# A hybrid encoder layer on one core: the next input's loads move to GpSimd, and two groups of the first pass go last, by seven products

## The chip, the cores and the metric

The kernel runs on one core of a Trainium2 chip. The metric is the device time in microseconds (us) of one execution; of several runs the median is given. TensorE (PE) multiplies matrices, with a queue of weight loads beside it (PEld); VectorE (DVE), ScalarE (ACT) and GpSimd (POOL) do elementwise work; SyncE (SP) issues most transfers (DMAs); GpSimd and ScalarE issue some. Every engine works through its own list of instructions in order, and waits for others by semaphores. An instruction that waits holds up all that stands behind it on its engine.

## The reference

One encoder layer over 2048 tokens of width 1024:

```python
y = rmsnorm(h, norm_mix_g) @ w_in                      # q, k, v (512 each) and two halves of 512 for the convolution
att = dilated_sliding_attention(q, k, v)               # 8 heads, 3 patterns (window, dilation): (128,1) (512,4) (2048,16)
conv = conformer_conv(a, g, conv_w, ...)               # gated, 31 taps along the tokens, layernorm, silu
h = h + concatenate([att, conv]) @ w_out
h = h + softmax(xq xk^T / 16) xv @ w_xo                # cross-attention to 256 memory tokens, 4 heads
u = rmsnorm(h, norm_mlp_g) @ w_up                      # 1024 -> 4096
h = h + square(relu(u)) @ w_down                       # 4096 -> 1024
out = rmsnorm(h, norm_final_g)
```

All is in float32. The kernel keeps each operand as two fp16 parts, a high and a low one, and makes a product of three matmuls (`mm3`: high·high, high·low, low·high; lines 374 to 376). In the profile a name that ends in h or l is such a part.

## The kernel before

**Stages.** First the memory tokens are projected and x is normalised and transposed (to about 130 us), then come the linear layers for q, k, v and the convolution's input, and the first attention (to about 670 us). Then the 2048 tokens go in four passes of 512 (`post(p)`), each with the same stages: the mixed input times `w_out` (matmuls called `o`), the scores of cross-attention (`xs`), its output (`x`), the MLP, and the final norm. TensorE's products in these stages are `x[features] x tokens`: a weight tile of 128×128 is loaded, and 512 or 256 tokens stream through it.

**The MLP.** The 4096 hidden columns are eight groups of 512. Two groups are made (`up`), then multiplied by `w_down` (`dn`), four times in a pass. `orders[p]` says in which order the groups come. A group is made in one of two ways. A *whole* group takes four weight tiles of 1024×128 (`ws_u`), 96 matmuls of 512 columns on a plain input `y` (in pass 0), or 192 of 256 columns on an input in block columns (the whole groups of pass 1). The other way, `quad`, treats weights and input as 2×2 blocks and takes seven products in place of eight (Strassen's scheme): weights that were combined in advance lie in DRAM as `ust[fg][0..6]` and come as tiles `ws_t`, and the input comes in block columns B11, B12, B2, T1, T32, T4, of 256 tokens each, that hold blocks and sums of blocks. Seven products are 168 matmuls of 256 columns. `columns` makes those tiles and `put_columns` fills them, on VectorE and ScalarE, while the stage `x` runs.

**Weights.** In pass 0 a weight comes from DRAM in float32 (`raw_u`, `raw_d`), is split in two parts by ScalarE (L361) and VectorE (L362) into one of four buffers, and for later passes some are saved to DRAM (`wst`). In later passes they are loaded from `wst` or `ust` into one of seven buffers (`wtile`). The combined weights are made by `prep`, a generator with 24 steps in pass 0: it loads two tiles `pw`, forms sums on VectorE, splits them on ScalarE (L1548) and VectorE (L1551), and stores the parts (`give`, `step`). In pass 0 it prepares groups 0 and 1, whose stores SyncE issues; in passes 1 and 2 the other six, with GpSimd's issues. The first group by seven products before this change is in pass 1.

**Side work.** While TensorE does pass p, the attention (`att`) and the convolution (`conv`) of the tokens of pass p+1 are woven in: `weave` takes one step of the main generator and then, for each side, as many steps as its rate says. Their results are stored to DRAM (`cath`, `catl`, from tiles `cacc`, `cth`, `lhl`), and `load_pair` loads them back as the input of the next pass, 16 loads of 128 KB for each pass; a load waits for its store to land. They are issued by SyncE (a load reads cath<-cath in the profile, a store cath<-cacc).

**The early linear layers.** `lead` starts the first two of the units (`glu`: a scale for the weights, a load, a split) while the memory's last products still run, and `pipeline` goes on with the rest, with some steps ahead of each unit's products. `done` says how many steps the first two have had.

The order of the instructions on each engine is set when the program is built: a scheduler simulates a timeline and places each instruction, so a change at one place can move rows at another. The lines that the change touches are those of `pipeline`, `lead`, `att`, `load_pair`, `columns`, `quad`, and the loops of `post`.

Of the kernel before, what the change touches and what calls it, by code (L numbers as in the profile page):

```python
# [34 lines left out]
KC = D // P  # L35
# [13 lines left out]
def hybrid_layer(ctx, tc, A, out):  # L49
    nc = tc.nc  # L50
    ACT, DVE, POOL, PE = nc.scalar, nc.vector, nc.gpsimd, nc.tensor
# [5 lines left out]
    def dma(o, i, q=None):  # L57
        return (q or nc.sync).dma_start(o, i)
# [634 lines left out]
            if k < KC - 1:  # L693
                yield

    def pipeline(*units, done=0):

        def go(i, n=1):
            for _ in range(n if i < len(units) else 0):
                next(units[i])  # L700

        for i, n in enumerate((4, 3, 1)):
            go(i, n - done if i < 2 else n)
        for i, u in enumerate(units):
# [265 lines left out]
    with ExitStack() as st:  # L970
        sp = pool("stage", stack=st)
        setup0()
        mg = memory(sp)
        next(mg)
        next(mg)
        setup()
        xp = xprep(sp, (0, 1))
        alln = tuple(range(NG))
        early01 = (0, 1)
        weave(islice(mg, 12), (xp, 0.34))  # L980
        weave(islice(mg, 23), (xp, 0.65))
        units = [u for c in range(3) for u in glu(c, early01)]
        units += [lin_qk(isq, c) for c in range(4) for isq in (False, True)]

        def lead():

            next(units[0])
            next(units[1])
            for u in units[:2]:
                next(u)  # L990
                next(u)
                yield

        weave(mg, (xp, 0.65), (lead(), 0.5))
        drain(xp)
        banks["mm"] = (0, 1, 2, 5, 6)
        steps = pipeline(*units, *glu(3, early01), lin_v(0, alln), lin_v(1, early01), done=3)
        qkl = qk_load()
        next(steps)
        later = xprep(sp, (2, 3))  # L1000
        weave(islice(steps, 9), (later, 2.2), (qkl, 1.2))
        drain(later, qkl)
# [146 lines left out]
    cats = {}  # L1149
# [74 lines left out]
    def att_units(p, far, then):  # L1224
# [78 lines left out]

        load_v(0, (2, 1, 0) if far else (0, 1))
        nxt = None if far else load_keys(0, p)
        if p == 1:
            yield None
        for pr in range(H // 2):
            o0 = aq.tile([P, 4, 2, ROW], F32, tag="o0", name=f"o0_{p}{pr}", bufs=2)
# [110 lines left out]
    with ExitStack() as st:  # L1420
# [5 lines left out]
        rest = pinned(pipeline(*frest[:2], lin_v(1, (2, 3), True, True), *frest[2:], ahead(0), ahead(1), done=2), "pe")  # L1426
        for _ in range(38):
            next(rest)

# [72 lines left out]
    def load_pair(p, half, j):  # L1502
        for q, src in (("h", cath), ("l", catl)):
            for e in range(2):
                k = 4 * (1 - half) + 2 * j + e
                dma(cats[p][q, k], src[k][:, 512 * p:512 * (p + 1)])

    def resid_linear(load, rhs, korder, resid, hs, ssum, scale, gains, y, name, steps=False, wide=False, put=None):

# [89 lines left out]

    ready = set()  # L1600
    preps = {0: (0, 1), 1: (3, 5, 6, 7), 2: (4, 2)}
    orders = {0: range(8), 1: (0, 1, 2, 4, 3, 5, 6, 7), 2: (0, 1, 3, 5, 6, 7, 4, 2)}
    whole = {0: tuple(range(8)), 1: (2, 4), 2: ()}
    prepping = {}

    def columns(p):

        names = {"B11": 0, "T1": 1, "T4": 2}
        if p == 1:
            names["B12"] = 7  # L1610
        one = {(n, q): yp.tile([P, 4, 256], F16, tag=f"y{q}{i}", name=f"{n}{q}{p}") for n, i in names.items() for q in "hl"}
        two_ = {(n, q): [yp.tile([P, 2, 2, 256], F16, tag=f"y{q}{i + x}", name=f"{n}{q}{p}{x}") for x in range(2)]
# [46 lines left out]
    def quad(p, fg, src, sink, rsb):  # L1659

        def tile(i):
            t = wtile(f"t{p}{fg}{i}", 7, (P, 8, P))
            dma(flat(t), ust[fg][i])
            return t
# [50 lines left out]
    def post(p):  # L1715
# [72 lines left out]
                yield  # L1788
        banks["S"] = (3, 4)

        src = put = None
        if p:
            one, two_, src = columns(p)
            put = put_columns(one, two_, hs)
            y = None
        else:
            y = ytiles("m")
        ssum = ssum_tile(f"x{p}")
        xl = resid_linear(lambda m: wpost(bscr[m], f"b{p}{m}", S_B), pr_, list(range(KC)), lambda m: hs[m], hs, ssum, K_B,
                          gxm[:, 8:16], y, f"x{p}_", True, put=put)  # L1800
        for _ in range(3):
            next(xl)
            if late:
# [38 lines left out]
        for g in range(FG // 2):  # L1842
# [3 lines left out]
            for i, fg in enumerate(fgs):  # L1846
# [5 lines left out]
                ks = (0, 1, 2, 3, 4, 5, 6, 7)  # L1852
                if fg not in whole[p]:
                    while fg not in ready:
                        next(prepping[p])
                    yield from main_quad or quad(p, fg, src, into(ht), rsb)
                    ks = (0, 1, 2, 3, 6, 7, 4, 5)
                    continue
                for c in range(4):
                    wh, wl = wpost(wcols(w_up, fg * 512 + c * P), f"u{p}{fg}_{c}", S_UP, (P, 8, P),  # L1860
                                   4 * fg + c if fg in whole[1] else None, p)
                    pt = ps("mm", "up")
                    for z in range(2 if src else 0):
                        for k in range(KC):
                            n = f"B{1 + k // 4}{1 + z}"
                            mm3(halved(pt)[:, z], wh[:, k, :], wl[:, k, :], src[n]("h", k % 4), src[n]("l", k % 4),
                                k == 0, k == KC - 1)
                    for k in range(0 if src else KC):
                        mm3(pt, wh[:, k, :], wl[:, k, :], y["h", k], y["l", k], k == 0, k == KC - 1)

                    def finish(pt, j):

# [228 lines left out]
    for p in range(NG):  # L2101
# [8 lines left out]
        if p + 1 < NG:  # L2110
# [67 lines left out]
```

## Time and profile before

| | |
|---|---|
| median of 3 runs | 2642.85 us (2641.27 to 2646.11) |
| the profiled execution's own time | 2648.63 us |
| its span | 2646.4 us |
| TensorE busy | 2588.9 us, 98% |
| VectorE, ScalarE, GpSimd busy | 1946.5, 1241.8, 279.9 us |
| mean granted clock of TensorE | 0.993 |
| pass 0: `o` from 668, `x` from 771, first `up` from 821, `dn` from 868, 961, 1058, 1151 | us from the span's start |
| pass 1: `x` from 1338, first `up` from 1382, last `dn` from 1659 | us |

The profile is one execution. "Idle before" is time in which an engine stood still ahead of an instruction, with the work that released it. Matmuls overlap, so a matmul of 512 columns is recorded as 0.38 us long, while the next one starts 0.22 us after it.

### The profile page before, as it was taken

The numbers are of one execution on the slowest core, as the hardware profiler recorded it, in microseconds if no ns is written. First come the engines' busy times: TensorE is split into PE (matmuls) and PEld (weight loads), VectorE is DVE, ScalarE is ACT, GpSimd is POOL, SyncE is SP. The second block draws the span as 40 slices with busy tenths as digits, with TensorE's granted clock in tenths as the row PEclk, the third lists the DMA queues.
The fourth block names the chain that finished last, engine by engine and source line by source line (L and its number), as shares of the span: only waits on it lengthen the run. The fifth ranks groups of instructions, "written<-read, shape, count | busy, mean of one in ns | idle before, by whom it ended". The sixth has DMA issues, their size and how long they took to land. (4 is left out here: it accounts for less than half of the span.)

```text
span 2646.4 us, 45524 instructions
## 1 busy us (share of the span) xinstructions
PE 2588.9 (98%) x17710; PEld 1650.2 (62%) x17710; DVE 1946.5 (74%) x3775; ACT 1241.8 (47%) x2194; POOL 279.9 (11%) x369
## 2 busy tenths in 40 slices
PE   7999999999999999999999999999999999999998
PEld 7844448767555545545576677455776664468876
DVE  5896656567767999775799996467899556675566
ACT  5747545476555344554553344256443234452323
POOL 1134101132100010100011111000110000000000
PEclk9999999999999999999999999999999999999999
DMA  8987968666634757885367678454686465345442
GB/s 264 297 271 218 289 227 260 193 183 180 177 102 133 212 171 221 237 271 172 112 212 218 194 237 253 143 163 131 215 263 192 141 207 167 97 135 168 159 137 80
DMA packets 406361, 509.51 MB, mean 193 GB/s; under 512 B 81181, under 2 KB 301265, under 8 KB 405376
## 3 DMA queue, kind: packets, MB, share of 16 engines
q1 hardware_dynamic: 387728, 452.64, 56.4%
q0 software_dynamic: 13232, 44.94, 5.3%
q10 hardware_dynamic: 5184, 9.01, 0.9%
q8 instruction: 139, 2.28, 0.4%
q14 instruction: 78, 0.64, 0.1%
HBM read 390.75 MB, written 115.75 MB: 191 GB/s over the span
## 5 line engine op out<-in xcount | busy, mean ns | idle before, releaser
L391 DVE SCALAR_TENSOR_TENSOR cacc<-cu,cw,cacc 128x512 f32<-128x512 f32 x480 | 364.2, 764 | 5.4
L374 PE MATMUL dn<-hhh,ws_d 128*128 128x512 f16 x768 | 289.0, 381 | 8.7 <-DMA ws_d<-wst 5.6
L375 PE MATMUL dn<-hhl,ws_d 128*128 128x512 f16 x768 | 291.6, 381 | 0.6 <-DVE hhl L1655 0.6
L376 PE MATMUL dn<-hhh,ws_d 128*128 128x512 f16 x768 | 291.3, 381 | 0.0
L1039 DVE CUSTOM_DVE_ANT_0 sm<-s,mask,qks 128x256 f32<-128x256 f32 (+1 forms) x384 | 150.8, 433 | 35.4 <-PE s L1080 31.1
L1040 ACT ACTIVATE sm<-sm,o 128x256 f32<-128x256 f32 (+1 forms) x288 | 119.4, 455 | 112.1 <-DVE o L1039 111.7
L1050 DVE TENSOR_TENSOR pl<-pt,ph 128x512 f16<-128x512 f32 x160 | 109.5, 684 | 45.8 <-ACT ph L1049 45.4
L1049 ACT CAST ph<-pt 128x512 f16<-128x512 f32 x160 | 91.7, 573 | 101.1 <-PE pt L1046 101.0
L1903 DVE SCALAR_TENSOR_TENSOR h<-dn,bd,h 128x512 f32<-128x512 f32 x96 | 71.4, 745 | 83.5 <-PE dn L376 83.0
L375 PEld LDWEIGHTS <-ws_t 128*128 128x128 f16 x1232 | 120.7, 98 | 18.6 <-issue 3.0
L376 PEld LDWEIGHTS <-ws_d 128*128 128x128 f16 x768 | 75.3, 98 | 90.6 <-issue 2.5
L374 PEld LDWEIGHTS <-ws_t 128*128 128x128 f16 x1232 | 120.9, 98 | 17.3 <-DMA ws_t<-ust 0.6
L376 PEld LDWEIGHTS <-ws_t 128*128 128x128 f16 x1232 | 120.8, 98 | 17.1 <-issue 1.1
L374 PEld LDWEIGHTS <-ws_d 128*128 128x128 f16 x768 | 75.3, 98 | 88.4 <-DMA ws_d<-wst 5.8
L375 PEld LDWEIGHTS <-ws_d 128*128 128x128 f16 x768 | 75.7, 99 | 84.2 <-issue 2.3
L1046 PE MATMUL pt<-ident,sm 128*128 128x128 f32 x640 | 97.7, 273 | 4.7 <-ACT sm L1040 2.6
L1686 ACT ACTIVATE e<-e 128x512 f32<-128x512 f32 x88 | 55.2, 630 | 95.5 <-DVE e L1684 95.5
L374 PE MATMUL up<-T32h,ws_t 128*128 128x256 f16 x352 | 96.8, 275 | 2.8 <-ACT e L1678 2.8
L374 PE MATMUL o<-cath,ws_o 128*128 128x512 f16 x256 | 97.3, 382 | 0.5 <-ACT cath L1218 0.3
L375 PE MATMUL o<-catl,ws_o 128*128 128x512 f16 x256 | 97.8, 382 | 0.0
L375 PE MATMUL up<-T32l,ws_t 128*128 128x256 f16 x352 | 96.8, 275 | 1.0 <-DVE T32l L1642 1.0
L375 PE MATMUL xs<-ws_a,yh 128*128 128x512 f16 x256 | 97.0, 379 | 0.3 <-DVE ws_a L362 0.2
(558 smaller groups left out, 7716.8 us busy)
## 6 DMA issues: line engine op xcount, KB each, us to landing
ws_t<-ust SPq DMA_DIRECT2D x154, 512.0 KB
ws_d<-wst SPq DMA_DIRECT2D x80, 512.0 KB
ust<-pt POOLq DMA_DIRECT2D x36, 512.0 KB, 4.8
scan<-in_w_up_dram SPq DMA_DIRECT2D x32, 512.0 KB
scan<-in_w_down_dram SPq DMA_DIRECT2D x32, 512.0 KB
raw_o<-in_w_out_dram SPq DMA_DIRECT2D x32, 512.0 KB
raw_a<-ascr SPq DMA_DIRECT2D x32, 512.0 KB
raw_b<-bscr SPq DMA_DIRECT2D x32, 512.0 KB
```

The lines of the kernel that those rows point to most:

```text
L374: PE.matmul(o, lh, rh, start=first, stop=False, skip_group_check=more)
L375: PE.matmul(o, lh, rl, start=False, stop=False, skip_group_check=more)
L376: last["pe"] = PE.matmul(o, ll, rh, start=False, stop=end, skip_group_check=more)
L391: DVE.scalar_tensor_tensor(acc, u[:, t:t + 512], cw[:, c, t:t + 1], acc, op0=ALU.mult, op1=ALU.add)
L1039: last["dve"] = DVE.tensor_tensor_reduce(dst, so, mask[:, 256 * m:256 * m + nk], SCORE, 3e38, ALU.add, ALU.min, mn)
L1040: last["act"] = ACT.activation(dst, dst, AF.Exp, bias=mn, scale=-1.0)
L1046: last["pe"] = PE.transpose(pt[:, j, :], sm[:, j, :], ident)
L1049: ACT.copy(ph, pt)
L1050: DVE.tensor_tensor(pl, pt, ph, op=ALU.subtract)
L1686: ACT.activation(e, e, AF.Square)
L1903: last["dve"] = DVE.scalar_tensor_tensor(hs[m], pt, K_DN, hs[m], op0=ALU.mult, op1=ALU.add)
```

## The change

It has three parts.

1. `load_pair` issues its loads on GpSimd in place of SyncE, for all passes.
2. In pass 0 the groups come in the order 2 to 7, 0, 1. Groups 0 and 1 are made by seven products. The upper input is in block columns in pass 0 too, so the six whole groups take matmuls of 256 columns. `prep` starts six steps of the main generator sooner, at rate 1.0 in place of 0.9. A tile for seven products first stores weights that are still unsaved.
3. In `lead` the second unit's two steps become one and come after the first unit's; `pipeline` takes a number of steps for each of the two units. Pass 1's attention yields two empty steps at its start in place of one.

```diff
-    def pipeline(*units, done=0):
+    def pipeline(*units, done):
...
-            go(i, n - done if i < 2 else n)
+            go(i, n - done[i] if i < 2 else n)
...
             next(units[0])
             next(units[1])
-            for u in units[:2]:
-                next(u)
-                next(u)
-                yield
+            next(units[0])
+            next(units[0])
+            yield
+            next(units[1])
+            yield
...
-        steps = pipeline(*units, *glu(3, early01), lin_v(0, alln), lin_v(1, early01), done=3)
+        steps = pipeline(*units, *glu(3, early01), lin_v(0, alln), lin_v(1, early01), done=(3, 2))
...
-        if p == 1:
+        for _ in range(2 if p == 1 else 0):
             yield None
...
-                dma(cats[p][q, k], src[k][:, 512 * p:512 * (p + 1)])
+                dma(cats[p][q, k], src[k][:, 512 * p:512 * (p + 1)], POOL)
...
-    orders = {0: range(8), 1: (0, 1, 2, 4, 3, 5, 6, 7), 2: (0, 1, 3, 5, 6, 7, 4, 2)}
-    whole = {0: tuple(range(8)), 1: (2, 4), 2: ()}
+    orders = {0: (2, 3, 4, 5, 6, 7, 0, 1), 1: (0, 1, 2, 4, 3, 5, 6, 7), 2: (0, 1, 3, 5, 6, 7, 4, 2)}
+    whole = {0: (2, 3, 4, 5, 6, 7), 1: (2, 4), 2: ()}
...
-        if p == 1:
+        if p < 2:
             names["B12"] = 7
...
         def tile(i):
+            save(0)
             t = wtile(f"t{p}{fg}{i}", 7, (P, 8, P))
...
-        src = put = None
-        if p:
-            one, two_, src = columns(p)
-            put = put_columns(one, two_, hs)
-            y = None
-        else:
-            y = ytiles("m")
+        one, two_, src = columns(p)
+        put = put_columns(one, two_, hs)
...
-                        next(prepping[p])
+                        next(prepping[p], None)
...
-                    for z in range(2 if src else 0):
+                    for z in range(2):
...
-                    for k in range(0 if src else KC):
-                        mm3(pt, wh[:, k, :], wl[:, k, :], y["h", k], y["l", k], k == 0, k == KC - 1)
...
-            weave(islice(main, 4 if p else 27), *sides)
-            sides.append((prepping[p], 1.2 if p else 0.9))
+            weave(islice(main, 4 if p else 21), *sides)
+            sides.append((prepping[p], 1.2 if p else 1.0))
```

**How the rows move.** SyncE at the end of pass 1, before. The `ws_d` tiles are the weights of the last down-projection, `ws_t` those of the group by products ahead of it.

```order
L58 DMA ws_t_18713<-ust_6_237 128x2048
L58 DMA catl_107<-cacc_2_15056 128x512
L58 DMA cu_3_20593<-uscr_71 128x542
L58 DMA cath_100<-cacc_2_15834 128x512
L58 DMA cath_18750<-cath_99 128x512
L58 DMA catl_18751<-catl_107 128x512
L58 DMA ws_d_0_18760<-wst_174 128x2048
L58 DMA catl_108<-cacc_2_15834 128x512
L58 DMA cath_18750<-cath_100 128x512
L58 DMA cath_101<-cacc_2_16449 128x512
L58 DMA ws_d_0_18762<-wst_178 128x2048
```

The same place on SyncE in the changed kernel:

```order
L58 DMA ws_t_19500<-ust_6_237 128x2048
L58 DMA cu_3_21380<-uscr_71 128x542
L58 DMA cath_100<-cacc_2_16621 128x512
L58 DMA catl_108<-cacc_2_16621 128x512
L58 DMA ws_d_0_19547<-wst_174 128x2048
L58 DMA cath_101<-cacc_2_17236 128x512
L58 DMA ws_d_0_19549<-wst_178 128x2048
```

The loads of the next input (cath_18750<-cath_99 and its like) are gone from between the `ws_d` loads; the stores are still there. On GpSimd, at the end of pass 1 in the changed kernel, the loads of the first pieces stand ahead of the last stores of combined weights:

```order
L58 DMA ust_5_236<-pt_71_18949 128x2048
L58 DMA cath_19793<-cath_94 128x512
L58 DMA cath_19793<-cath_95 128x512
L58 DMA cath_19793<-cath_96 128x512
L58 DMA catl_19794<-catl_102 128x512
L58 DMA catl_19794<-catl_103 128x512
L58 DMA catl_19794<-catl_104 128x512
L58 DMA ust_3_234<-pt_71_18989 128x2048
```

Before, GpSimd's two `ust` rows followed each other with none of the loads between. SyncE at the end of pass 0 in the changed kernel, where the second group's combined weights are stored and loaded back (the numbers behind `ust` count tiles: 0_189 to 6_195 are the second group's):

```order
L58 DMA ws_t_13775<-ust_2_191 128x2048
L58 DMA ws_t_13843<-ust_5_194 128x2048
L58 DMA v_20_14476<-vtok 128x1x1040 x2
L58 DMA ust_3_192<-pt_11_13585 128x2048
L58 DMA ld_13665<-oscr_1_89 128x4x132
L58 DMA ust_6_195<-pt_11_13588 256x1x512
L58 DMA ws_t_13777<-ust_3_192 128x2048
```

The load of ws_t_13777 waits for the store of ust_3_192 four rows ahead of it. That store waits for VectorE, whose rows there are these:

```order
L1684 TENSOR_TENSOR e_13582<-e_13582,up 128x512
L1684 TENSOR_TENSOR e_13618<-e_13618,up 128x512
L1686 SCALAR_TENSOR_TENSOR e_13582<-e_13582,ssumx_9534 128x512
L1552 SCALAR_TENSOR_TENSOR pt_11_13585<-pw_11_13269,bd,pt_11_13585 128x512
L1552 SCALAR_TENSOR_TENSOR pt_11_13585<-ps_11_13396,bd,pt_11_13585 128x512
L1552 SCALAR_TENSOR_TENSOR pt_11_13588<-pw_11_13269,bd,pt_11_13588 128x512
```

The rows e are results of the first group by products; the last piece `pt` is made behind them. (The changed kernel's line 1552 is line 1551 of the kernel before.)

More of the change, by code (lines that the diff above doesn't have):

```diff
@@ L1425, in hybrid_layer @@
         lbv = pool("far_v", stack=st)
-        rest = pinned(pipeline(*frest[:2], lin_v(1, (2, 3), True, True), *frest[2:], ahead(0), ahead(1), done=2), "pe")
+        rest = pinned(pipeline(*frest[:2], lin_v(1, (2, 3), True, True), *frest[2:], ahead(0), ahead(1), done=(2, 2)), "pe")
         for _ in range(38):
@@ L1789, in post @@
         banks["S"] = (3, 4)
-        src = put = None
-        if p:
-            one, two_, src = columns(p)
-            put = put_columns(one, two_, hs)
-            y = None
-        else:
-            y = ytiles("m")
+        one, two_, src = columns(p)
+        put = put_columns(one, two_, hs)
         ssum = ssum_tile(f"x{p}")
         xl = resid_linear(lambda m: wpost(bscr[m], f"b{p}{m}", S_B), pr_, list(range(KC)), lambda m: hs[m], hs, ssum, K_B,
-                          gxm[:, 8:16], y, f"x{p}_", True, put=put)
+                          gxm[:, 8:16], None, f"x{p}_", True, put=put)
         for _ in range(3):
```

## The prediction

> **What bounds the kernel now.** I read the page first, then the windows of TensorE's low clock, then the timelines of TensorE and SyncE around the largest hole.
>
> ```profile
> PE 2588.9 (98%) x17710; PEld 1650.2 (62%) x17710; DVE 1946.5 (74%) x3775; ACT 1241.8 (47%) x2194; POOL 279.9 (11%) x369
> PE 32%; DVE 4%; DMA 2%; issue 1%; ACT 1%; POOL 0%; SPq 0%; POOLq 0%; DVEq 0%; ACTq 0%
> L374 PE MATMUL dn<-hhh,ws_d 128*128 128x512 f16 x768 | 289.0, 381 | 8.7 <-DMA ws_d<-wst 5.6
> ```
>
> TensorE works for 98% of the span and leads the chain of waits. So only two things count: TensorE's own work, and the few places where it stands still. The last row names one: 5.6 us of standing before down-projections, for a weight load. The windows show that standing has a second price, a low clock behind it (the columns are window, length, PE busy, PEld, DVE, ACT, POOL, granted clock, DMA share, GB/s).
>
> ```profile
> 675.00:685.00 10.00, 7.29 (x53) 4.28 (x51) 5.87 (x17) 3.35 (x8) 0.00 (x0) 0.83 0.88 146
> 966.00:976.00 10.00, 7.66 (x41) 3.46 (x40) 9.93 (x17) 3.57 (x6) 0.20 (x1) 0.83 0.46 132
> 1655.00:1668.00 13.00, 8.52 (x33) 3.57 (x34) 2.14 (x4) 1.25 (x2) 0.00 (x0) 0.87 0.81 253
> 132.00:150.00 18.00, 14.76 (x59) 7.10 (x58) 17.39 (x48) 7.75 (x11) 3.97 (x4) 0.81 1.06 350
> ```
>
> A clock of 0.83 over 10 us loses 1.7 us, 0.87 over 13 us also 1.7, 0.81 over 18 us 3.4. At 966 and 675 TensorE is idle 2.3 and 2.7 us, so a hole of that size costs about 4 us in all. [...]
>
> The largest hole, on TensorE and then on SyncE's queue:
>
> ```profile
> 1653.65 0.27 PE L376 MATMUL up<-B2h,ws_t 128*128 128x256 f16 x1
> 1659.48 0.61 PE L374 MATMUL dn<-hhh,ws_d 128*128 128x512 f16 x1 [5.56 <-DMA ws_d<-wst]
> 1662.44 0.51 PE L375 MATMUL dn<-hhl,ws_d 128*128 128x512 f16 x1
> ```
>
> ```profile
> 1641.10 0.32 SPq L58 DMA_DIRECT2D cath<-cath  x1
> 1642.47 0.39 SPq L58 DMA_DIRECT2D catl<-cacc  x1
> 1643.95 0.42 SPq L58 DMA_DIRECT2D cath<-cath  x1
> 1647.55 0.32 SPq L58 DMA_DIRECT2D catl<-catl  x1
> 1647.96 0.38 SPq L58 DMA_DIRECT2D ws_d<-wst  x1
> 1650.31 0.55 SPq L58 DMA_DIRECT2D ws_d<-wst  x1
> 1653.73 0.32 SPq L58 DMA_DIRECT2D catl<-catl  x1
> 1654.80 0.38 SPq L58 DMA_DIRECT2D ws_d<-wst  x1
> ```
>
> SyncE issues in order. A row catl<-catl or cath<-cath loads a piece of the next pass's input that was stored a moment before (catl<-cacc), so it waits for that store to land: SyncE stands from 1644.37 to 1647.55 and again up to 1653.73. The ws_d loads of the last down-projection stand behind. The one that the first dn matmul needs goes out at 1654.80, and the matmul starts at 1659.48, 4.7 us later: the landing of 512 KB. The first eight dn matmuls then run 0.43 us apart instead of 0.22.
>
> **The change, part by part.**
>
> *The input loads go to GpSimd.* In the new order of SyncE no cath<-cath or catl<-catl stands between the ws_d loads; only the stores do, and their data comes from DVE, which works 2.1 us in the whole window from 1655. The first ws_d load would go out at about 1644 to 1648. TensorE is ready for it at 1653.9, so the hole of 5.56 and its low clock of 1.7 go: −7.3. Bounds: if ws_d goes out only 2 us sooner, −2; no gain needs ws_d to be held by DMA transfers, which the rival below prices. GpSimd takes 16 issues per pass. What stands behind them on GpSimd:
>
> ```profile
> 1612.82 0.61 POOL L58 DMA_DIRECT2D ust<-pt  x1 [4.60 <-DVE lcol L350]
> 1617.46 1.34 POOL L58 DMA_DIRECT2D ust<-pt  x2 [4.03 <-DVE pt L1551]
> ust<-pt POOLq DMA_DIRECT2D x36, 512.0 KB, 4.8
> 1621.18 8.06 SPq L58 DMA_DIRECT2D ws_t<-ust  x4
> ```
>
> In pass 1 six of the loads stand ahead of the last two ust stores (1617.46). The lower ones overwrite a tile that the store of 1612.82 reads, so they wait some 5 us for it, and six issues of about 0.6 us follow: the stores move to about 1622, land by 1629 at the 4.8 to 7 us that such stores take. The ws_t that reads them stood on SyncE until 1629 anyway, and TensorE uses it after 1640. I cost this at nothing, covered by about 10 us. In the same passes the loads themselves are wanted only by the next pass's first matmuls, some 40 us on.
>
> [...]
>
> *Pass 0's upper products.* The pitch of a 512-column matmul and of a 256-column one come from two stretches without a hole, of 17 and 46 matmuls:
>
> ```profile
> 899.68 0.38 PE L375 MATMUL dn<-hhl,ws_d 128*128 128x512 f16 x1
> ...
> 903.13 0.38 PE L376 MATMUL dn<-hhh,ws_d 128*128 128x512 f16 x1
> ```
>
> ```profile
> 1428.41 0.27 PE L374 MATMUL up<-B11h,ws_u 128*128 128x256 f16 x1
> ...
> 1433.33 0.27 PE L374 MATMUL up<-B2h,ws_u 128*128 128x256 f16 x1
> ```
>
> (903.13 − 899.68)/16 = 0.2157 us and (1433.33 − 1428.41)/45 = 0.1093. A group of 512 hidden columns is 4×8×3 = 96 matmuls of 512 columns, 20.71 us. Six groups now take 192 of 256 columns: 20.99, so +0.28 each, +1.7. The two groups by seven products take 7×24 = 168: 18.36, so −2.35 each, −4.7. Sum −3.0.
>
> *What this asks of VectorE.* Pass 0 now makes its upper input in block columns, and prepares both groups' weights sooner.
>
> ```profile
> 771.00:821.00 50.00, 49.20 (x308) 26.50 (x306) 36.47 (x71) 29.80 (x56) 0.20 (x1) 1.00 0.44 121
> 868.00:1058.00 190.00, 187.66 (x1082) 95.49 (x1081) 185.36 (x297) 82.78 (x126) 14.67 (x20) 0.99 0.69 203
> 1058.00:1191.00 133.00, 133.00 (x703) 65.38 (x701) 101.33 (x161) 71.31 (x97) 10.64 (x10) 1.00 0.83 254
> ```
>
> ```profile
> L1531 DVE SCALAR_TENSOR_TENSOR ml<-h,gxm,mh 128x512 f16<-128x512 f32 x1 | 0.7, 747 | 0.0
> L1642 DVE TENSOR_TENSOR T32l<-t,T32h 128x512 f16<-128x512 f32 x4 | 2.7, 680 | 0.0
> L1637 DVE SCALAR_TENSOR_TENSOR t<-h,gxm,yv 128x256 f32<-128x256 f32 x4 | 1.9, 475 | 0.0
> L1646 DVE TENSOR_TENSOR T4l<-yv,T4h 128x256 f16<-128x256 f32 x4 | 1.7, 414 | 0.0
> L1551 DVE SCALAR_TENSOR_TENSOR pt<-pw,bd,pt x16: 741/1010/1278, 1024.4 to 1166.9; 128x1024 f16<-128x1024 f32 x8, 128x512 f16<-128x512 f32 x8
> ```
>
> Block columns: the upper four tiles take 0.41 + 3×0.475 each, the lower four 2×0.475 + 2×0.68 + 2×0.414, together 19.9 us, in place of eight splits of 0.747, 6.0: about +14. In the stage from 771 VectorE is idle 13.5 us, so that stage is full and a little runs over. From 868 to 1058 it is busy 185.4 of 190. Preparing two groups is about 30 us of VectorE work, which ran from about 1020 to 1167. It must now end by the second of the two groups, about 1120, and starts six steps of the main work sooner at a slightly higher rate: of 24 steps of 1.25 us each some seven, 8 us, move into the full stretch, which has 4.6 us free. Against it the two groups by products come last, where 32 us are free, and need no weight splits. What does not fit, 8 − 4.6 = 3.4 us, can be taken from convolution work that TensorE doesn't wait for, or not. So TensorE's loss is 0 to 6 us, its low clock included (two holes as at 966 would be 8, but one is there already); I take +2.
>
> *The entry of the two groups, at the end of pass 0.* Two chains are new. First: the tiles for the first two products use the buffers that the down-projection just ahead still reads; between the release and the use TensorE has some 4 us of other products, and a 512 KB load takes 4.7 from issue to use (above), so about 1 us is missing. Second: the last prepared piece of the second group is made on VectorE behind four rows of the first group's results, stored by SyncE and loaded back: three rows of 0.745 us, a store of 4.8, a load of 4.7 and two issues of 0.4 are 12.5 us. TensorE's work between those rows and the product that needs the piece is four products of 24×0.1093 = 2.62 us and some attention, about 11.4. So about 1 us is missing there too. In this stretch the DMA share is 0.83, and 14 loads of 512 KB (7 MB) replace 8 (4 MB), so either can take longer. Together 0 (covers a little longer than counted) to +10 (both chains 3 us late, each with a low clock of 1.7); I take +2.5.
>
> *The lead.* At the first linear units the second scale's work leaves VectorE's and TensorE's way by one step.
>
> ```profile
> 135.25 0.38 PE L203 MATMUL p<-wsc,onesq 128*128 128x1 f32 x2 [1.94 <-DVE p2s L207]
> 139.10 0.61 PE L374 MATMUL lin<-xh,ws_g 128*128 128x512 f16 x1 [1.04 <-ACT ws_g L361]
> ```
>
> The wait of 1.94 is for the first scale, in the way of six matmuls of 1.5 us that need nothing of it; now they go first. But VectorE is busy 17.4 of 18 us there (window 132 above), so ws_g is ready at about the same time, and the wait at 139.10 grows by most of what the other loses. 0 to −3 (both holes shrink and the low clock goes with them); I take −1. The second empty step of pass 1's attention changes no row of TensorE's order up to the hole at 679, so that hole stays: 0.
>
> Sum: −3.0 − 7.3 − 1 + 2 + 2.5 = −6.8. Against the profiled execution's 2648.63 us (span 2646.4 and 2.2 around it) that is 2641.8. That execution lies 5.8 above the median of the runs, 2642.85, and I forecast for the median: 2636. A measurement of this kernel can tell about 0.2%, 5.3 us, from no change.
>
> **The rivals.**
>
> *Slower: the prepared pieces come late.* If the store and load of the last piece take 7 us each in the crowded stretch, as GpSimd's store of 1617.46 did (up to 7), the second chain is 12.5 + 4.5 = 17 us against 11.4: a hole of 5.6 and 1.7 of clock. If the buffers' chain adds 3 + 1.7 and VectorE's overload 4, it is +16 in place of +4.5, and the time is 2642.85 − 11.3 + 16 = 2647.6; with a second late product (the fifth waits for a load queued behind the late one), 2650. It decides against the change from about 7 us for each landing on. For it speaks the DMA share of 0.74 to 0.90 behind 1058; against it, that quads in pass 1 and 2 fetch such tiles with no hole of this kind, except at 1659.
>
> *No difference: VectorE.* If the 3.4 us and the overflow of the block columns all reach TensorE, with two more holes as at 966, it is +8 in place of +2: 2642.
>
> *The hole at 1659 isn't SyncE's.* DMA is busy 0.81 there at 253 GB/s. If ws_d, issued sooner, only shares the engines with more transfers, 2 of the 7.3 us are won: 2641.5. Against it: the load took 4.7 us even there.
>
> [...]
>
> *More: the holes near 966 and the lead close.* The new order shifts both; −4 and −2 more: 2630.
>
> **How the numbers follow.** Forecast, 2631 to 2640: 0.42, of which 0.06 lies above 2637.6. More: 0.14. VectorE: 0.12, all within 0.2%. SyncE's hole stays, or GpSimd's issues: 0.10, within. Late pieces, 2645 to 2653: 0.22, of which 0.18 above 2648.1. So faster 0.36 + 0.14 and a little of the third, 0.53; within 0.2%, 0.28; slower 0.19. The range leaves out the tails of the first and the last: 2627 to 2650.
>
> **What would show it.** In the changed kernel: no hole above 2 us near 1650 to 1660, and ws_d rows on SyncE without a stretch of standing; up matmuls of 128x256 in pass 0; the span from pass 0's first up product to its last dn about 3 us shorter plus its holes; ws_t<-ust as the releaser of a hole near 1105 to 1130 where the late pieces are right; VectorE above 98% busy from 820 to 1060 with releasers hhh or rl where that rival is. The prediction is wrong if pass 0 gains holes of over 6 us, or the dn at pass 1's end still waits for ws_d.

## The result: slower by 0.2%, and the profile after

The changed kernel takes 2650.47 us (median of 22 runs, 2643.60 to 2660.15), the kernel before 2645.34 beside it (22 runs). The ratio is 1.0021, with a 95% interval of 1.0014 to 1.0028: slower by some 5.6 us, where 2636 was forecast. Of the 14.5 us between, 2.5 are the base: the three runs that the forecast started from had a median of 2642.85. The profile below is of an execution of 2645.35 us, 5 us below its median; a second profile, further down, is of one of 2650.36.

The page of the changed kernel, its lines on the engines and on the groups that wait:

```profile
PE 2584.8 (98%) x18430; PEld 1721.8 (65%) x18430; DVE 1952.4 (74%) x3807; ACT 1245.5 (47%) x2214; POOL 305.7 (12%) x417
L374 PE MATMUL dn<-hhh,ws_d 128*128 128x512 f16 x768 | 288.0, 379 | 1.8 <-DVE e L1684 1.1
L374 PE MATMUL up<-T32h,ws_t 128*128 128x256 f16 x384 | 105.2, 274 | 9.8 <-DMA ws_t<-ust 7.1
```

Matmuls are 720 more, as the arithmetic has it (6×96 + 2×72). The wait of the down-projections for ws_d, 5.6 us, is gone; a wait of 7.1 us for ws_t stands at the upper products. The prediction named a hole of over 6 us in pass 0 as a sign that it was wrong. TensorE's timeline at the end of pass 1, then at the end of pass 0 (a bracket is the idle time before the row, with what ended it):

```profile
1657.24 0.27 PE L376 MATMUL up<-B2h,ws_t 128*128 128x256 f16 x1
1657.35 0.38 PE L374 MATMUL dn<-hhh,ws_d 128*128 128x512 f16 x1
```

```profile
1102.59 0.19 PE L1057 MATMUL opt<-v,pl 128*128 128x65 f16 x1
1105.97 0.28 PE L374 MATMUL up<-B11h,ws_t 128*128 128x256 f16 x1 [3.19 <-DMA ws_t<-ust]
...
1140.71 0.40 PE L374 MATMUL up<-T32h,ws_t 128*128 128x256 f16 x1 [7.13 <-DMA ws_t<-ust]
1140.90 0.42 PE L375 MATMUL up<-T32l,ws_t 128*128 128x256 f16 x1
```

At 1657 TensorE goes from the upper products to the down-projection without a stop. At 1106 it waits 3.2 us for the first tile of the first group by products, and at 1140.7 it waits 7.1 us for a tile of the second. The matmuls behind the second hole start 0.19 to 0.21 us apart, in place of 0.11: the clock is at half. In the windows view of both profiles of the changed kernel (granted clock third from the end), the first profile:

```profile
1100.00:1112.00 12.00, 8.81 (x84) 7.25 (x82) 8.69 (x15) 5.82 (x10) 1.76 (x3) 1.00 0.92 294
1136.00:1153.00 17.00, 12.29 (x92) 10.18 (x93) 8.08 (x22) 6.63 (x11) 2.16 (x4) 0.80 0.79 250
```

and the second:

```profile
1104.00:1116.00 12.00, 8.96 (x74) 7.02 (x73) 8.20 (x14) 5.29 (x8) 1.76 (x3) 0.86 0.95 301
1139.00:1156.00 17.00, 11.48 (x82) 9.29 (x83) 6.99 (x20) 6.14 (x10) 2.16 (x4) 0.80 0.71 229
```

These windows hold part of each hole too, where TensorE has no work for a low clock to slow. Windows of 1 us around the second hole, from the first profile, show when the low clock begins and ends:

```profile
1135.00:1136.00 1.00, 0.00 (x0) 0.00 (x0) 0.00 (x0) 0.00 (x0) 0.00 (x0) 1.00 0.26 89
1138.00:1139.00 1.00, 0.00 (x0) 0.00 (x0) 1.00 (x3) 0.25 (x1) 1.00 (x3) 0.79 0.75 287
1145.00:1146.00 1.00, 1.00 (x9) 0.82 (x8) 0.00 (x0) 0.18 (x1) 0.00 (x0) 0.80 0.86 291
```

It is at half for 6.8 us, from 1138.6 to 1145.4 (0.50 in each of the six windows between), and TensorE works for the last 4.7 of them, so it loses half of that, 2.3 us (17×0.20 = 3.4 would count the hole's end as well). In the second profile it is 2.6. The first hole loses nothing to the clock in the first profile and 1.5 in the second. So the entry of the two groups costs 3.2 + 7.1 + 2.3 = 12.6 us in the first and, with holes of 3.0 and 6.2, 3.0 + 1.5 + 6.2 + 2.6 = 13.3 in the second.

Why the tile is late is seen on VectorE and SyncE of the first profile. VectorE makes the last prepared piece:

```profile
1124.59 0.74 DVE L1552 SCALAR_TENSOR_TENSOR pt<-pw,bd,pt 128x512 f16<-128x512 f32 x1
1125.26 0.74 DVE L1552 SCALAR_TENSOR_TENSOR pt<-ps,bd,pt 128x512 f16<-128x512 f32 x1
```

SyncE stores it and loads it back:

```profile
1122.54 1.12 SPq L58 DMA_DIRECT2D v<-vtok  x2
1126.06 0.32 SPq L58 DMA_DIRECT2D ust<-pt  x1
1129.98 0.37 SPq L58 DMA_DIRECT2D ld<-oscr  x1
1130.45 0.58 SPq L58 DMA_DIRECT2D ust<-pt  x1
1136.54 1.68 SPq L58 DMA_DIRECT2D ws_t<-ust  x3
```

From the store's issue to the load's issue it is 10.5 us (SyncE's waits show 5.4 of them as waiting for ust<-pt to land), and from there to the matmul 4.2.

What the store waits for is not a crowd on the DMA engines alone: in its last 3 us their share is 0.20 to 0.28 (the window of 1135 above is one). The trace notes sixteen landings for such a store. Of this one eleven come within 2.6 us of its issue, one at 4.6, and the last four at 9.2 to 10.4. Just ahead of it SyncE issued two loads v<-vtok of 260 KB (the row at 1122.54); for each the trace notes five landings only, the last four at 7.0 to 8.3 and at 10.3 to 12.1 us. So it goes in all fourteen traces of this case: the 22 stores of 512 KB that SyncE issued within 6 us of such a pair landed in 7.1 to 13.3 us, the other 146 in 2.6 to 8.1. That the last parts of the store stand behind these loads is what the rows say, but no run moves the loads, so it was not shown by an edit.

### The profile page after: what moved, and what is told of

Read it like the earlier page. It is cut to its first block, busy times and chain, and to the rows that moved or that the text cites. A ratio compares the mean times of both kernels' runs of the same rounds, so it can differ in the third digit from the quotient of the medians.

```text
span 2643.2 us, 47068 instructions
## 1 busy us (share of the span) xinstructions
PE 2584.8 (98%) x18430; PEld 1721.8 (65%) x18430; DVE 1952.4 (74%) x3807; ACT 1245.5 (47%) x2214; POOL 305.7 (12%) x417
## 4 chain that ended last, share of the span: by engine, by line
PE 77%; DVE 11%; DMA 6%; issue 2%; ACT 2%; POOL 0%; SPq 0%; DVEq 0%; POOLq 0%; ACTq 0%
PE dn L375 7%; PE dn L374 7%; PE dn L376 7%; PE up L374 5%; PE up L376 5%; PE up L375 5%; PE lin L376 4%; PE lin L374 4%; PE lin L375 4%; DVE cacc L391 3%; PE x L374 2%; PE x L375 2%; PE x L376 2%; PE xs L375 2%; PE o L374 2%
## 5 line engine op out<-in xcount | busy, mean ns | idle before, releaser
L374 PEld LDWEIGHTS <-ws_t 128*128 128x128 f16 x1344 | 132.0, 98 | 29.8 <-DMA ws_t<-ust 11.0
L375 PEld LDWEIGHTS <-ws_t 128*128 128x128 f16 x1344 | 131.9, 98 | 22.3 <-issue 5.3
L376 PEld LDWEIGHTS <-ws_t 128*128 128x128 f16 x1344 | 131.8, 98 | 17.3
L374 PE MATMUL up<-T32h,ws_t 128*128 128x256 f16 x384 | 105.2, 274 | 9.8 <-DMA ws_t<-ust 7.1
L1684 DVE TENSOR_TENSOR e<-e,up 128x512 f32<-128x512 f32 x96 | 65.0, 682 | 60.7 <-ACT e L1680 39.6
L1680 ACT COPY e<-up 128x512 f32<-128x512 f32 x96 | 55.3, 582 | 114.6 <-PE up L376 114.1
L376 PE MATMUL up<-T32h,ws_t 128*128 128x256 f16 x384 | 105.3, 274 | 0.0
L375 PE MATMUL up<-T32l,ws_t 128*128 128x256 f16 x384 | 105.2, 274 | 0.0
L376 PE MATMUL up<-B2h,ws_t 128*128 128x256 f16 x384 | 104.7, 273 | 0.0
```

What stands on the lines that cost most here:

```text
L374: PE.matmul(o, lh, rh, start=first, stop=False, skip_group_check=more)
L375: PE.matmul(o, lh, rl, start=False, stop=False, skip_group_check=more)
L376: last["pe"] = PE.matmul(o, ll, rh, start=False, stop=end, skip_group_check=more)
L1680: last["act"] = ACT.copy(e, pt)
L1684: DVE.tensor_tensor(e, e, pt, op=ALU.add)
```

## The experiments

All times are medians; each ratio is to runs of the kernel before beside it, with its 95% interval. The kernel before was at 2644.0 to 2644.6 in these, and at 2645.34 beside the changed kernel. A difference between two of these kernels is one of medians; where their ratios (1.0021 for the changed kernel) give another, it stands in brackets.

**The loads alone.**

```diff
 # kernel before
-                dma(cats[p][q, k], src[k][:, 512 * p:512 * (p + 1)])
+                dma(cats[p][q, k], src[k][:, 512 * p:512 * (p + 1)], POOL)
```

> The kernel before with only the next input's loads moved to GpSimd. Theory A (SyncE's queue held the weights up): no hole over 1.5 us between 1640 and 1670 and no low clock there, 5.6 + 1.7 = 7.3 us less than before, about 0.997 of it. Rival (the DMA engines are full there, or GpSimd's issues make other transfers late): a hole of 3 us or more remains, and the gain is 2 us or less, 0.999 to 1.000.

2637.39 us, ratio 0.9972 (0.9963 to 0.9982), 7.1 us less. SyncE at the end of pass 1, and the first dn matmul:

```profile
1638.95 0.47 SPq L58 DMA_DIRECT2D ws_d<-wst  x1
...
1643.01 1.60 SPq L58 DMA_DIRECT2D ws_d<-wst  x3
```

```profile
1649.93 0.39 PE L374 MATMUL dn<-hhh,ws_d 128*128 128x512 f16 x1 [0.17 <-DMA ws_d<-wst]
```

The ws_d loads go out 11 us ahead of their use, and TensorE waits 0.17 us. Theory A holds in place and size. This kernel is faster than the one before and the changed one.

**The loads and the lead, without the products.** The third part of the change on top of the run above.

```diff
 # kernel before, loads on GpSimd
...
-            for u in units[:2]:
-                next(u)
-                next(u)
-                yield
+            next(units[0])
+            next(units[0])
+            yield
+            next(units[1])
+            yield
...
-        if p == 1:
+        for _ in range(2 if p == 1 else 0):
             yield None
```

> The kernel before with the loads moved to GpSimd and the change at the lead and at pass 1's attention, without anything in pass 0's products. It prices the third part. Theory: 0 to 3 us less than with the loads alone, 1 most likely; the wait for the first scale, 1.9, goes, and the wait for the first split weights grows. Rival: the same time within 1 us, or more by the moved attention step.

2638.58 us, ratio 0.9979 (0.9970 to 0.9988), against 0.9972 with the loads alone: no gain, 1.2 us more (1.9), which the intervals don't tell from nothing. Its timeline at the lead, from an execution 6 us above its median:

```profile
133.89 0.63 PE L541 MATMUL xt<-ident,xn 128*128 128x128 f32 x4 [0.48 <-DVE xv L546]
136.38 0.39 PE L374 MATMUL lin<-xh,ws_g 128*128 128x512 f16 x1 [1.87 <-ACT ws_g L361]
138.70 0.61 PE L376 MATMUL lin<-xh,ws_g 128*128 128x512 f16 x1 [0.69 <-DVE p2s L209]
```

The wait of 1.94 for the first scale is gone, the wait for ws_g has grown from 1.04 to 1.87, and a third one stands behind it.

So the products in pass 0 are what is left between this run and the changed kernel: 2650.5 − 2638.6 = 11.9 us (11.1).

**Block columns without products.**

```diff
 # changed kernel
-    orders = {0: (2, 3, 4, 5, 6, 7, 0, 1), ...
-    whole = {0: (2, 3, 4, 5, 6, 7), ...
+    orders = {0: range(8), ...
+    whole = {0: tuple(range(8)), ...
...
-            weave(islice(main, 4 if p else 21), *sides)
-            sides.append((prepping[p], 1.2 if p else 1.0))
+            weave(islice(main, 4 if p else 27), *sides)
+            sides.append((prepping[p], 1.2 if p else 0.9))
```

> The changed kernel with all eight groups of pass 0 whole and in the old order, preparation at its old start and rate, the upper input still in block columns. It prices the block columns. Theory A: the matmuls cost 8 x 0.28 = 2.2 us, VectorE's 14 us more are hidden but for 0 to 2; with the loads' gain of 7.3 and 1 of the lead: 4 to 6 us less than before. Rival C: new holes for VectorE between 820 and 1060 of 5 us or more, and no gain over before.

2639.20 us, ratio 0.9988 (0.9979 to 0.9998). Its median is 0.6 us above the run of loads and lead, its mean 1.8: about the 2.2 us of the 256-column matmuls, with VectorE's 14 us more hidden. Theory A's 4 to 6 us less than before are 5.3 between the medians, and 3.2 by the ratio. VectorE's holes of this profile lie elsewhere (2.1 and 1.5 us near 1134) than between 820 and 1060.

**The products, with the loads on SyncE.**

```diff
 # changed kernel
-                dma(cats[p][q, k], src[k][:, 512 * p:512 * (p + 1)], POOL)
+                dma(cats[p][q, k], src[k][:, 512 * p:512 * (p + 1)])
```

> The changed kernel with the input's loads issued by SyncE again. Theory A (the two new chains at the end of pass 0 cost what they cost, whoever issues the loads): the holes at the entry of the two groups stay at about 3 and 7 us, the hole at the end of pass 1 comes back, together 7.3 us more than the changed kernel. Rival B (GpSimd's 14 loads share the DMA engines with the late store, which took 10.4 us to land): the store lands in 5 to 7 us, the second hole falls to 0 to 3 us, and the time is within 3 us of the changed kernel's, the two effects in balance.

2648.26 us, ratio 1.0014 (1.0006 to 1.0023). The store of the late piece took 8.6 us from its issue to the load's, in place of 10.5 and, in the second profile of the changed kernel, 10.0:

```profile
1129.87 0.32 SPq L58 DMA_DIRECT2D ust<-pt  x1
1133.82 0.58 SPq L58 DMA_DIRECT2D ust<-pt  x1
1138.43 0.80 SPq L58 DMA_DIRECT2D ws_t<-ust  x2
```

The second hole is 4.8 us here, and a hole for ws_d of 2.5 us is back at the end of pass 1, smaller than in the kernel before. Neither side got its numbers whole: the store did not fall to 5 to 7 us and the hole not under 3, but the time came out as rival B has it, 2.2 us from the changed kernel's, and the loads, worth 7 us alone, are worth nothing that the intervals show beside the products.

**Only pass 1's loads on SyncE.**

```diff
 # changed kernel
-                dma(cats[p][q, k], src[k][:, 512 * p:512 * (p + 1)], POOL)
+                dma(cats[p][q, k], src[k][:, 512 * p:512 * (p + 1)], POOL if p > 1 else None)
```

> The changed kernel with the loads for pass 1 issued by SyncE and those for passes 2 and 3 by GpSimd. Theory B (at the end of pass 0 the loads from GpSimd share the DMA engines with the late store): second hole about 4.8 us in place of 7.1, as with all loads on SyncE, no hole at the end of pass 1; 2 to 5 us less than the changed kernel, 2646 to 2648. Rival (the difference of the two second holes is chance): the changed kernel's time within 1.5 us.

2644.60 us, ratio 1.0005 (0.9994 to 1.0015): 5.9 less than the changed kernel (4.2), where theory B said 2 to 5. The store took 8.1 us (1136.83 to 1144.94) and the second hole was 4.4. So GpSimd's loads beside the late store cost it about 2 us, and its hole as much or a little more. For the rest no line accounts; the profile is of an execution 5.6 us above the median.

**Other buffers for the first group.**

```diff
 # changed kernel, quad
             save(0)
+            if (p, fg, i) == (0, 0, 0):
+                turn_w[0] += (4 - turn_w[0]) % 7
             t = wtile(f"t{p}{fg}{i}", 7, (P, 8, P))
```

> The changed kernel with the weight tiles of the first group by products in pass 0 placed in other buffers (the rotation starts at the fifth of seven, not at one that the down-projection just ahead still reads). Theory A: the hole at the entry, 3.2 us, is gone, the second one stays; 3 to 5 us less than the changed kernel. Rival: the loads that now go out sooner push other transfers back, or the tile behind them waits instead, and less than 1.5 us is won.

2642.90 us, ratio 0.9997 (0.9987 to 1.0008), 7.6 less than the changed kernel (6.3), more than expected. The profile, of an execution 6.8 us below the median, goes into the first product without a stop:

```profile
1100.06 0.38 PE L376 MATMUL dn<-hhh,ws_d 128*128 128x512 f16 x1
1100.28 0.27 PE L374 MATMUL up<-B11h,ws_t 128*128 128x256 f16 x1
```

The hole at the entry is gone; the one at the second group stays, at 6.2 us. So the choice of buffers brought the first hole. Its 3.2 us do not account for all of the gain.

**The pieces prepared early.**

```diff
 # changed kernel
-            sides.append((cg, 0.85 if p else 1.0))
-            weave(islice(main, 4 if p else 21), *sides)
-            sides.append((prepping[p], 1.2 if p else 1.0))
+            sides.append((cg, 0.85 if p else 0.92))
+            weave(islice(main, 4 if p else 6), *sides)
+            sides.append((prepping[p], 1.2 if p else 0.8))
```

> The changed kernel with the preparation of pass 0 started 15 steps sooner at rate 0.8 (done some 8 steps sooner) and the convolution at rate 0.92 in place of 1.0. Theory A (the late piece makes the large hole at the second group): that hole, 7.1 us and its 3.4 of low clock, is gone, the entry's hole of 3.2 stays; 8 to 10 us less than the changed kernel, about 2641. Rival C (VectorE is what is short; moving preparation forward only moves the holes to the groups before): holes for VectorE between 820 and 1060 grow by 5 us or more, and the time stays within 3 us of the changed kernel's.

2640.82 us, ratio 0.9994 (0.9983 to 1.0005), 9.7 less than the changed kernel (7.1), about as theory A has it. No hole for ws_t is left, not at the entry either. Rival C is half right: VectorE's holes between 1019 and 1042 grow from 2.7 us (2.0 and 0.7) to 4.7 (2.7, 0.7 and 1.2), and two of 2.1 us come at 1089 and 1145.

**The same, with less VectorE work.**

```diff
 # run with early pieces, conv_unit
-            DVE.scalar_tensor_tensor(acc, u[:, t:t + 512], cw[:, c, t:t + 1], acc, ...)
+            if n != 1 or t % 2:
+                DVE.scalar_tensor_tensor(acc, u[:, t:t + 512], cw[:, c, t:t + 1], acc, ...)
```

> The changed kernel with the pieces prepared early (as in the run with early pieces) and every second tap of the convolution in pass 0 left out: 60 VectorE operations of 0.76 us, 46 us, less between about 870 and 1110, so the output of the second pass is not the reference's. Theory C (what is left of the loss is VectorE's: holes of 2.7, 0.7, 1.2, 2.1 and 2.1 us with VectorE as releaser and a low clock): these holes fall to under 3 us in all, and the time is 7 to 11 us below the run with early pieces, 2630 to 2635. Rival (they come from the order of the rows, an operation late behind others that itself wait for TensorE): over half of the holes stay, and less than 3 us is won.

2634.74 us, ratio 0.9967 (0.9954 to 0.9980), 6.1 below the run with early pieces (7.1): nearer to theory C's 7 to 11 than to the rival's 3. The stretch of six groups and the one of the last pair, first with early pieces, then with less convolution (PE is the first busy time, DVE the third):

```profile
863.00:1053.00 190.00, 185.22 (x1434) 130.85 (x1433) 184.00 (x293) 86.91 (x128) 17.16 (x19) 0.99 0.73 216
1053.00:1153.00 100.00, 95.78 (x691) 64.12 (x689) 72.04 (x123) 44.71 (x70) 20.80 (x26) 0.97 0.72 231
```

```profile
863.00:1053.00 190.00, 189.61 (x1490) 133.75 (x1488) 156.30 (x251) 90.30 (x133) 21.84 (x22) 1.00 0.75 221
1053.00:1153.00 100.00, 95.75 (x684) 64.27 (x683) 66.05 (x115) 45.29 (x72) 18.55 (x26) 0.98 0.75 244
```

With VectorE at 156 us in place of 184, TensorE gains 4.4 us in the first stretch: its holes there came from VectorE's load. In the second it gains nothing; a wait of 3.1 us for ScalarE's copy of a product (e) stands there now.

**One group by products.**

```diff
 # changed kernel
-    orders = {0: (2, 3, 4, 5, 6, 7, 0, 1), ...
-    whole = {0: (2, 3, 4, 5, 6, 7), ...
+    orders = {0: (1, 2, 3, 4, 5, 6, 7, 0), ...
+    whole = {0: (1, 2, 3, 4, 5, 6, 7), ...
```

> The changed kernel with only group 0 by seven products in pass 0 (order 1 to 7, 0; seven whole groups). Theory A (the late prepared piece of the second group makes the large hole): no wait for combined weights over 2 us but the one at the entry, 7.1 + 3.4 us of hole and low clock gone, 2.6 us of matmuls more: about 8 us less than the changed kernel. Rival C (the loss is VectorE's, by block columns and the earlier preparation): within 3 us of the changed kernel.

2655.59 us, ratio 1.0040 (1.0026 to 1.0055): 5 us slower than the changed kernel, against theory A; with five runs the intervals leave room for rival C's 3 us. The wait for weights is gone, as A said. In its place stand many small ones between 960 and 1290, of 0.5 to 2.2 us, nearly all for VectorE or ScalarE. Three of the groups from the lines view of that stretch (after the last bar the idle time before, and its releaser):

```profile
L374 PE MATMUL dn<-hhh,ws_d 128*128 128x512 f16 x192 | 72.4, 379 | 3.1 <-ACT ws_d L361 1.8 <-ACT hhh L1871 1.3
L376 PE MATMUL up<-B11h,ws_u 128*128 128x256 f16 x52 | 14.2, 273 | 2.1 <-DVE ws_u L362 2.1
L1057 PE MATMUL opt<-v,pl 128*128 128x65 f16 x72 | 8.5, 192 | 2.4 <-DVE pl L1051 2.4
```

A whole group late in the pass keeps its eight weight splits on ScalarE and VectorE, while the preparation still comes early. That this is why the holes are more was not tried apart.

**Products of weights that need no preparation.**

```diff
 # changed kernel
-            dma(flat(t), ust[fg][i])
+            dma(flat(t), ust[fg][i] if p else wst[(8, 9, 10, 11, 16, 17, 18)[i]])
...
-                    while fg not in ready:
+                    while p and fg not in ready:
...
-            weave(islice(main, 4 if p else 21), *sides)
-            sides.append((prepping[p], 1.2 if p else 1.0))
+            weave(islice(main, 4 if p else 27), *sides)
+            sides.append((prepping[p], 1.2 if p else 0.9))
```

> The changed kernel, but the two groups by products of pass 0 take other weights that were saved long before (so the output of pass 0 is not the reference's), and the preparation has its old start and rate. The same products, loads and buffers, without the wait for a prepared piece and without the earlier VectorE work. Theory A: no hole at the second group, about 10.5 us less than the changed kernel, and with the early VectorE work gone another 0 to 3: 2637 to 2640. Rival (the loads of 7 MB in place of 4 in a crowded stretch): holes for ws_t of 5 us or more remain, 2645 or more.

2652.44 us, ratio 1.0035 (1.0024 to 1.0046). The second hole is gone, as A said; but the first one is larger, and the time is the rival's:

```profile
1114.15 0.39 PE L374 MATMUL up<-B11h,ws_t 128*128 128x256 f16 x1 [8.30 <-DMA ws_t<-wst]
```

```profile
SPq L58 <- PE up L376: 4.9, 1, 4.9
SPq L58 <- DMA ws_t<-wst: 4.4, 2, 3.2
```

The second fence is SyncE's waits from 1085 to 1122: its longest is 4.9 us for TensorE to release a buffer. Another hole of 4.0 us, for VectorE, stands ahead of the down-projection. So the run agrees with the early pieces that the late piece made the second hole, but it doesn't price the rest, because the order at the entry came out anew.

**A second profile of the changed kernel.**

> The changed kernel once more, for a second profile of it. The first one was of an execution 5 us below the median. If the holes at the entry of the two groups vary from execution to execution, they or the low clock behind them are larger here, in the sum 13 to 19 us where the first profile has 13.7. If they are the same, the variation lies elsewhere.

2650.36 us. The entry costs 13.3 us in place of 12.6, so the 5 us between the two executions lie mostly elsewhere. At the lead the clock is 0.81 over 18 us here and 0.91 there, up to 1.8 us more; over the whole span it is 0.993 here and 0.996 there. A hole for VectorE at 1043 is 2.1 us in place of 0.7, and some others differ by tenths.

**All remedies together.** Early pieces, other buffers, pass 1's loads on SyncE, and the lead and the attention's start as before.

```diff
 # run with early pieces
-                dma(cats[p][q, k], src[k][:, 512 * p:512 * (p + 1)], POOL)
+                dma(cats[p][q, k], src[k][:, 512 * p:512 * (p + 1)], POOL if p > 1 else None)
...
+            if (p, fg, i) == (0, 0, 0):
+                turn_w[0] += (4 - turn_w[0]) % 7
...
+            for u in units[:2]:
+                next(u)
+                next(u)
+                yield
```

> The changed kernel with all that helped it: the pieces prepared early, other buffers for the first group by products, pass 1's input loads on SyncE again and those of passes 2 and 3 on GpSimd, and the lead and the attention's start as in the kernel before. It asks whether products in pass 0 can pay. Theory A: no hole for ws_t over 1.5 us at the entry; VectorE's holes of 5 to 9 us stay; 2636 to 2640, no better than the loads alone (2637.4). Rival (the remedies add up: 9.7 of the early pieces, 7.6 of the buffers, 5.9 of the loads): below 2634.

2645.62 us, ratio 1.0002 (0.9993 to 1.0012): worse than with early pieces alone, against both. No hole for ws_t is left, but VectorE's and ScalarE's are back at 966 (2.2 and 0.8 us), 1048 (1.6) and 1072 (1.2), and a new one stands in the last pair's down-projection:

```profile
1160.69 1.44 PE L374 MATMUL dn<-hhh,ws_d 128*128 128x512 f16 x3 [5.21 <-ACT hhh L1654]
```

So no version with products in pass 0 that computes the reference came below the loads alone.

## Why the prediction was wrong, point by point

*The loads: right.* −7.3 forecast; the loads alone measured −7.1. The hole's cause was SyncE's queue. The DMA share at the end of pass 1 is no lower in the changed kernel (0.83 in the 18 us from 1650) and the hole is gone all the same, which is against the rival that the engines were full. The move took waits for landing out of the weights' queue: before, two waits of SyncE for catl<-cacc to land, 5.5 us together, fell between 1641.5 and 1654. The hole behind them and its low clock, 5.6 + 1.7 us, account for the whole gain. What the prediction left out is that at another place, the end of pass 0, the same loads from GpSimd lie beside a store that is waited for, and cost it about 2 us. The chance of 0.10 also counts GpSimd's issues; no run shows them late: GpSimd's stores ust<-pt landed in 4.8 us (median) in the kernel before and in 5.0 in the changed one, with VectorE busy for 74% of the span in both.

*The matmuls: −3.0, not contradicted.* Their count is as worked out, and block columns alone cost 0.6 (means: 1.8) where 2.2 was worked out.

*The entry of the two groups: the step that failed.* The two chains were named; their size was not: +2.5 taken, 0 to +10 given, 12.6 and 13.3 measured. The term that was most too small is the landing of the late store, 4.8 us and 0.4 for its issue, where the load behind it went out after 10.5. For the second chain the prediction set 12.5 us of chain against 11.4 of cover. In the profile the chain is 1124.59 to 1140.71, 16.1 us, and TensorE runs dry at 1140.71 − 7.13 = 1133.58, after 9.0 us of cover. The store's 4.8 us, a median over pass 1 and 2 and of GpSimd's queue, was the wrong row: this store stands on SyncE right behind two v<-vtok loads, and the order of SyncE's rows showed them there. For the first chain a load of 4.7 stood against 4 us of cover; the load went out at 1100.67 and was used at 1105.97, 5.3 us, with 2.1 us of cover left. SyncE shows no wait for TensorE just ahead of this load; the store before it (catl<-lhl) had waited 0.8 us for ScalarE, so SyncE's order may have a part in this hole too; no run shows how large. Each hole is a difference of two larger numbers, so errors of 0.6 to 3.6 us in them became holes of three and seven times the forecast, and the clock added 2.3 to 4.1, of which only the range's upper end had counted anything. The rival of late pieces, at a chance of 0.22, is what happened, and the time is just above its price (2647.6 to 2650). That it came so near is partly luck: its 7 us each for the store and the load were 10.5 and 4.2, and its 4 us for VectorE were less.

*VectorE: +2, in place about right and in size not far off.* The hole near 969 (2.3 and 1.7 of clock) is gone, and holes of 2.0 and 0.7 at 1022 and 1042, with a clock of 0.86 over the 12 us from 1018, come: 2.7 + 1.7 = 4.4 against 4.0. In the second profile the holes are 2.0 and 2.1, 5.8 with the clock. So it is +0.4 to +1.8 where +2 was taken. But VectorE is why the late piece can't simply be made sooner: with early pieces its holes come to 8.9 us, and taking 46 us of its work away brought 6.1 (7.1).

*The lead: −1, not found.* With the loads, the lead's change measured +1.2 (1.9), not told from zero. The first wait went and the second grew, as described; a third came that was not.

*The sum.* −7.1 (loads) + 1.2 (lead) + 11.9 (products) = +6.0; measured +5.1 between the medians of the 22 runs, and +5.6 by the ratio. The 11.9 was found as a difference, so that this sum comes out says nothing by itself. The lines give it apart: the entry's 12.6 to 13.3, less the 3.0 of the matmuls, plus VectorE's 0.4 to 1.8, is 10 to 12.

## What to carry to other kernels

A load that waited for a store held up all that stood behind it on SyncE's queue, 5.5 us in two waits at the end of pass 1; moved to a queue where nothing urgent followed, it gave back the whole hole here (5.56 us before, 0.17 with the loads alone). Work that is to be made, stored and loaded back just ahead of its use was priced too low by a median of other stores, 4.8 us: at this place it was 10.5 from the store's issue to the load's. So price it by the landing at its own place, with the transfers that its queue issued just before, and add the clock's fall behind the holes, 2.3 to 4.1 us at this entry. With VectorE at 97% of a stretch (184 of 190 us with early pieces), a rearrangement that saves TensorE 3 us of matmuls had 8.9 us of holes for VectorE, and remedies that each took away a hole did not add up (2645.62 us for all, 2640.82 for the early pieces alone): each set a new order of the rows, with holes at other places.

## What the runs showed of the hardware that was not expected

The same hole did not bring the same fall of the clock in two executions. The hole of 3.2 us at 1106 left the clock at 1.00 in one execution of the changed kernel and at 0.86 over 12 us in the other; at the lead the clock fell for 3.4 us in the one and for 6.8 in the other. In the first profile the clock is at half five times, for 3.41 us four times and for 6.83 once (the end of the program aside), and the five starts, at 46.3, 138.5, 541.3, 1022.5 and 1138.6, lie whole multiples of 3.41 us apart. On this grid the hole of 3.2 us is cut into 1.7 and 1.5 us in the first profile, and in the second, where it is 3.0, into 2.6 and 0.5; there the clock fell at the grid line behind the 2.6. So in this pair the hole's price in clock hung on where it fell.

And the late store of 512 KB took 8.1 to 12.3 us up to the load that waited for it in the five profiles in which a load waited for it so, where the median landing of GpSimd's stores in the page is 5.0. In all traces SyncE's stores of that size landed in 7.1 to 13.3 us where a pair of loads v<-vtok of 260 KB had been issued within 6 us ahead of them, and in 2.6 to 8.1 elsewhere; no run moves those loads.
